# Opening of a hybrid decoder block on one core: norm weights spread by a 128-row product, fewer steps to the first norm factors, v's first weights cast on GpSimd and VectorE

## Chip, cores and metric

One core of a Trainium2 chip runs the whole program. The metric is the device time of one execution in microseconds (us), lower is better. Of the kernel before, three executions were timed (1725.62 to 1727.33, median 1726.06), and a further one was profiled.

## The reference

One decoder layer on x of 1024 tokens by 1024 channels, in float32. Two token mixers run side by side on the same normed input and are merged with gates; a SwiGLU channel mixer follows. Cut to what the change touches, and what hangs on it:

```python
def rms_norm(x, w):
    xf = x.astype(jnp.float32)
    y = xf * lax.rsqrt(jnp.mean(xf * xf, axis=-1, keepdims=True) + EPS)
    return (y * w.astype(jnp.float32)).astype(x.dtype)
...
h = rms_norm(x, attn_norm_w[l])
proj = h @ w_in[l]
q, k, v, u, g = jnp.split(proj, splits, axis=-1)
...
x = x + (g_a * y_a + g_b * y_b) @ w_out[l]
h = rms_norm(x, ffn_norm_w[l])
gt, up = jnp.split(h @ w_gate_up[l], 2, axis=-1)
x = x + (jax.nn.silu(gt) * up) @ w_down[l]
```

The change lies in the first norm of this, `rms_norm(x, attn_norm_w)`, and in the first piece of the product with w_in: the 256 columns of v that are computed first.

## The kernel before

**Tiling.** The 1024 tokens are eight tiles of 128 rows (`xts[0]` to `xts[7]`). A tile is loaded, its rows are squared and summed (`squares`), the sums become factors 1/sqrt(mean + EPS) (`roots`, through `rstd_of` and `rsq`), the rows are multiplied by factor and norm weight (`norm`, L714), and TensorE transposes them in 128x128 blocks into PSUM (`turn_x`, L724). All products are made to float32 accuracy out of two parts of each operand: a high part, which is a cast to fp32r (`split_hi`, ScalarE, L120), and a low part, the rest (`split_lo`, VectorE, L125). So three products stand for one: high by high, low by high, high by low. `hT_hi` and `hT_lo` are the transposed tile's two parts, and `low_x` makes the second.

**The opening.** `opening()` runs the first 50 us or so. While tiles arrive one by one, it computes the first 256 columns of v for tile after tile (`v_tile`, L1110): 24 products of 128x256 for each tile, eight of each of the three kinds. For tile 0 their order is hT_hi by v's high weights, hT_lo by the high weights, hT_hi by the low weights. v's weights come in two halves of 512 rows (`raws[0]`, `raws[1]`, each 128x1024 in the memory on chip), with high parts `wv[0][0]`, `wv[1][0]` (tile name vwh) and low parts `wv[0][1]`, `wv[1][1]` (vwl). Before, ScalarE casts both high parts (`wv_hi`, L120), VectorE subtracts for the first low part (L125) and GpSimd for the second (L1137). Behind `v_tile(1)` and the next ones follow u's first weights and the long rest of the program.

**What sets the order.** The list handed to `steps` is the order: each entry is issued behind the last instruction issued so far on VectorE, ScalarE and TensorE (`in_order`, with `after`), so these three engines work in the order of the list. GpSimd isn't tied by it; its instructions run in their own order as soon as what they wait for is there. A tile's buffer or a weight buffer is loaded anew when its last reader has finished. Loads are issued by SyncE, ScalarE or GpSimd, each with a queue of its own in which transfers follow one another.

**The norm weights.** `attn_norm_w` is one row of 1024. It is loaded into row 0 of `wb` (tile anw_b, L199), and `spread_weights(g)` (L212, L213) multiplies a column of ones with 512 of it, a product over one row, and copies the result from PSUM over all 128 rows of `wb`. `keep_busy(n)` (L208) issues n products of a tile of ones, whose results nobody reads.

**The first factors.** For tile 0 ScalarE squares and sums the first 512 columns (L699) and VectorE the other 512 (L700), and an addition joins both sums (L703). `rstd_of` scales by 1/D and adds EPS (L682); `rsq` takes a square root on ScalarE (L652), a reciprocal on VectorE (L653) and four more VectorE steps (L654 to L657): one Newton step. For the other tiles ScalarE squares all 1024 columns (L696).

Of the kernel before, what the change touches and what calls it, by code (L numbers as in the profile page):

```python
# [10 lines left out]
F32 = mybir.dt.float32  # L11
F32R = mybir.dt.float32r
AF = mybir.ActivationFunctionType
ALU = mybir.AluOpType
AX = mybir.AxisListType

P = 128
S = 1024
D = 1024
# [7 lines left out]
EPS = 1e-6  # L27
# [30 lines left out]
def kernel(  # L58
# [27 lines left out]
    nc = tc.nc  # L86
    dve, act, pool, pe = nc.vector, nc.scalar, nc.gpsimd, nc.tensor
# [11 lines left out]
    sm = ctx.enter_context(tc.tile_pool(name="sm", bufs=4))  # L99
# [12 lines left out]
    def nm(s):  # L112
        uid[0] += 1
        return f"{s}_{uid[0]}"

    def f32(ap):
        return ap.bitcast(F32)

    def split_hi(dst, src):
        act.copy(dst, src)  # L120
# [3 lines left out]
    def split_lo(dst, src, hi):  # L124
        last_lo[0] = dve.tensor_tensor(dst, src, f32(hi), op=ALU.subtract).ins  # L125
# [64 lines left out]
        queue.dma_start(xts[i][:], xs[i * P : (i + 1) * P, :])  # L190


    one = ap.tile([1, P], F32, name="one", bufs=1)
    busy = ap.tile([P, 512], F32R, tag="vl", name="busy")
    dve.memset(f32(busy[:]), 1.0)
    dve.memset(one[:], 1.0)
    wb = ap.tile([P, D], F32, name="anw_b", bufs=1)
    anw = [wb[0:1, 512 * g : 512 * (g + 1)] for g in range(2)]
    nc.scalar.dma_start(wb[0:1, :], attn_norm_w[:, :])  # L199
    xts[0] = ap.tile([P, D], F32, tag="xt", name="xt0", bufs=4)  # L200
    for g, queue in enumerate((nc.sync, nc.scalar)):
        queue.dma_start(xts[0][:, 512 * g : 512 * (g + 1)], xs[0:P, 512 * g : 512 * (g + 1)])
# [441 lines left out]
    def rsq(v, n, fast):  # L644

        r = sm.tile([P, 16], F32, tag="r", name=nm("r"))[:, :n]
        t = sm.tile([P, 16], F32, tag="t", name=nm("t"))[:, :n]
        if fast:
            act.activation(t, v, AF.Ln)
            act.activation(r, t, AF.Exp, scale=-0.5)  # L650
        else:
            act.activation(t, v, AF.Sqrt)  # L652
            dve.reciprocal(r, t)  # L653
        dve.tensor_tensor(t, r, r, op=ALU.mult)  # L654
        dve.scalar_tensor_tensor(t, v, 3.0e38, t, op0=ALU.min, op1=ALU.mult)
        dve.tensor_scalar(t, t, -0.5, 1.5, op0=ALU.mult, op1=ALU.add)
        dve.tensor_tensor(r, r, t, op=ALU.mult)  # L657
        return r
# [21 lines left out]
    def rstd_of(ss, n, scale, fast=False):  # L680
        v = sm.tile([P, 16], F32, tag="v", name=nm("v"))[:, :n]
        dve.tensor_scalar(v, ss, scale, EPS, op0=ALU.mult, op1=ALU.add)  # L682
        return rsq(v, n, fast)
# [5 lines left out]
    def squares(tiles):  # L689

        ss = sqs[tiles] = sm.tile([P, 4], F32, tag="ssx", name=nm("ssx"), bufs=2)[:, : len(tiles)]
        for j, i in enumerate(tiles):
            junk = ap.tile([P, D], F32, tag="junk", name=nm("xj"), bufs=1)
            src = xts[i]
            if i:
                act.activation(junk[:], src[:], AF.Square, accum_out=ss[:, j : j + 1])  # L696
            else:
                s2 = sm.tile([P, 1], F32, tag="ss", name=nm("ss"), bufs=1)
                act.activation(junk[:, :512], src[:, :512], AF.Square, accum_out=ss[:, j : j + 1])  # L699
                dve.tensor_tensor_reduce(  # L700
                    junk[:, 512:], src[:, 512:], src[:, 512:], 1.0, 0.0, ALU.mult, ALU.add, accum_out=s2[:]
                )
                dve.tensor_tensor(ss, ss, s2[:], op=ALU.add)  # L703

    def roots(tiles):

        r = rstd_of(sqs.pop(tiles), len(tiles), 1.0 / D)
        for j, i in enumerate(tiles):
            rx[i] = r[:, j : j + 1]

# [19 lines left out]
    def low_x(i):  # L730
        for g in range(2):
            src4, h_ = turned.pop((i, g))
            split_lo(hT_lo[:, 4 * g : 4 * g + 4, i * P : (i + 1) * P], src4, h_)
# [350 lines left out]
    def opening():  # L1084
# [10 lines left out]
        halves = [[t_[:].rearrange("p (k c) -> p k c", c=256) for t_ in w] for w in wv]  # L1095
        uw, o = [], {}

        def wv_hi(g):
            split_hi(wv[g][0][:], raws[g][:])

        def v_tile(i, first=0, n=24):

            if i % 2 == 0 and not first:
                o[i // 2] = pg()
            ts, dst = slice(i * P, (i + 1) * P), o[i // 2][:, 256 * (i % 2) : 256 * (i % 2 + 1)]
            order = ((0, 0), (0, 1), (1, 0)) if i else ((0, 0), (1, 0), (0, 1))
            terms = [(k, a_, b_) for a_, b_ in order for k in range(NKT)]
            for n_, (k, a_, b_) in list(enumerate(terms))[first : first + n]:
                l_, r_ = (hT_hi, hT_lo)[a_][:, k, ts], halves[k // 4][b_][:, k % 4, :]
                last_mm[0] = pe.matmul(dst, l_, r_, start=n_ == 0, stop=n_ == len(terms) - 1).ins  # L1110
# [9 lines left out]
        def turn_low(i):  # L1120
# [9 lines left out]
            lambda: spread_weights(1),  # L1130
            lambda: norm(0),
            lambda: keep_busy(1),
            lambda: wv_hi(0),
            lambda: split_lo(wv[0][1][:], raws[0][:], wv[0][0][:]),
            lambda: turn_x(0, (0,)),
            lambda: wv_hi(1),
            lambda: pool.tensor_tensor(wv[1][1][:], raws[1][:], f32(wv[1][0][:]), op=ALU.subtract),  # L1137
            lambda: turn_x(0, (1,)),
            lambda: low_x(0),
            lambda: v_tile(0),  # L1140
            lambda: squares((1,)),
            lambda: roots((1,)),
# [996 lines left out]
```

## Time and profile before

| What | Value |
|---|---|
| time of the profiled execution | 1724.98 us |
| span from its first to its last instruction | 1723.2 us |
| median of three other executions | 1726.06 us (1725.62, 1726.06, 1727.33) |
| TensorE (PE) busy | 1713.9 us, 99% of the span |
| VectorE (DVE) busy | 1276.2 us, 74% |
| ScalarE (ACT) busy | 873.2 us, 51% |
| GpSimd (POOL) busy | 219.2 us, 13% |
| transfers | 281.64 MB, 163 GB/s on average |

How to read it: busy shares are those of one execution, with times in us from the span's start. The 1.78 us by which the execution is longer than its span lie around the program's instructions. Matmuls overlap, and their ends are modelled, so TensorE's busy share doesn't tell how close it is to its peak; the distance from one matmul's start to the next does. A row of the timeline gives start, length, engine, line of the kernel, operation, operands, and in brackets the idle time before it and what ended that. The chain that ended last is found from the last instruction backwards, each time to what released it. A line such as L125 is that of a helper, so the operands' names tell which step it is.

### The profile page before, as it was taken

What the parts mean: (1) busy time and instruction counts of PE and PEld (TensorE: products, weight loads), DVE (VectorE), ACT (ScalarE), POOL (GpSimd) and SP (SyncE); (2) the same over time, 40 slices, a digit from 0 to 9 for tenths busy, and PEclk for the clock granted to TensorE, in tenths of its full rate; (3) what the DMA queues carried; (4) which work ended last, traced back from release to release, by engine and by line L of the source; (5) the groups of instructions that cost most, each with busy time, mean ns of one, the idle gap of its engine ahead of it and who ended that gap; (6) DMA issues with size and microseconds to landing.
All of it is one profiled execution on the core that took longest, in us unless ns stands there. A gap on an engine that the chain in (4) does not pass through costs nothing.

```text
span 1723.2 us, 25849 instructions
## 1 busy us (share of the span) xinstructions
PE 1713.9 (99%) x9243; PEld 1478.2 (86%) x9243; DVE 1276.2 (74%) x2128; ACT 873.2 (51%) x1958; POOL 219.2 (13%) x207
## 2 busy tenths in 40 slices
PE   9999999999999999999999999999999999999999
PEld 7997889998998998988788888888888888888887
DVE  7675889898988987977677769966666666575544
ACT  6333335767877886865556325633333333333332
POOL 4997851000000000000000000000000000000000
PEclk9999999999999999999999999999999999999999
DMA  6344445436345345354863683244455445597663
GB/s 209 117 128 134 131 151 143 113 103 174 107 128 147 116 125 148 99 146 145 316 225 128 196 301 108 77 141 156 149 174 167 153 143 165 175 371 271 216 217 128
DMA packets 261603, 281.64 MB, mean 163 GB/s; under 512 B 16545, under 2 KB 181985, under 8 KB 261474
## 3 DMA queue, kind: packets, MB, share of 16 engines
q1 hardware_dynamic: 254160, 267.71, 48.4%
q0 software_dynamic: 5680, 9.39, 2.6%
q10 hardware_dynamic: 1634, 2.89, 0.5%
q8 instruction: 73, 1.20, 0.3%
q14 instruction: 56, 0.46, 0.1%
HBM read 181.84 MB, written 85.50 MB: 155 GB/s over the span
## 4 chain that ended last, share of the span: by engine, by line
PE 93%; DVE 2%; DMA 2%; ACT 1%; issue 1%; SPq 0%; DVEq 0%; ACTq 0%
PE acc L984 30%; PE acc L488 12%; PE pg L168 12%; PE pg L170 12%; PE pg L169 12%; PE wo L1854 3%; PE sc L1294 2%; PE sc L1293 2%; PE pT L1332 2%; DVE acc L594 1%; PE pg L1110 1%; PE pW L168 1%; PE pW L170 1%; PE pW L169 1%; PE pQ L819 1%; DMA room<-in_w_out_dram 1%
## 5 line engine op out<-in xcount | busy, mean ns | idle before, releaser
L594 DVE SCALAR_TENSOR_TENSOR acc<-u,cw,acc 128x1023 f32<-128x1023 f32 (+14 forms) x240 | 303.5, 1264 | 23.0 <-ACT acc L588 20.4
L168 PE MATMUL pg<-whi,hT_hi 128*128 128x256 f32 x704 | 199.2, 284 | 0.8 <-DVE v L125 0.8
L169 PE MATMUL pg<-wlo,hT_hi 128*128 128x256 f32 x704 | 199.9, 284 | 0.0
L170 PE MATMUL pg<-whi,hT_lo 128*128 128x256 f32 x704 | 199.9, 284 | 0.0
L125 DVE TENSOR_TENSOR wlo<-draw,whi 128x1024 fp32r<-128x1024 f32 x75 | 91.8, 1224 | 86.0 <-ACT whi L120 78.6
L120 ACT CAST whi<-draw 128x1024 fp32r<-128x1024 f32 x75 | 79.1, 1055 | 129.5 <-PE acc L488 121.0
L168 PEld LDWEIGHTS pg<-whi,hT_hi 128*128 128x128 f32 x704 | 133.8, 191 | 2.6 <-DVE v L125 1.0
L169 PEld LDWEIGHTS pg<-wlo,hT_hi 128*128 128x128 f32 x704 | 134.2, 191 | 1.7
L170 PEld LDWEIGHTS pg<-whi,hT_lo 128*128 128x128 f32 x704 | 134.3, 191 | 1.5
L120 ACT CAST whi<-wraw 128x1024 fp32r<-128x1024 f32 x90 | 94.7, 1053 | 71.1 <-PE pg L169 37.0
L488 PE MATMUL acc<-wlo,whi 128*128 128x512 f32 x308 | 119.8, 389 | 0.0
L488 PE MATMUL acc<-whi,wlo 128*128 128x512 f32 x308 | 119.8, 389 | 0.0
L168 PE MATMUL pg<-hT_hi,whi 128*128 128x512 f32 x288 | 114.5, 398 | 0.0
L170 PE MATMUL pg<-hT_hi,wlo 128*128 128x512 f32 x288 | 113.9, 395 | 0.0
L169 PE MATMUL pg<-hT_lo,whi 128*128 128x512 f32 x288 | 113.9, 395 | 0.0
L1300 ACT ACTIVATE E<-E,mn 128x640 f32<-128x640 f32 (+7 forms) x128 | 99.5, 777 | 26.0 <-DVE mn L1295 25.6
L120 ACT CAST whi<-s 128x1024 fp32r<-128x1024 f32 x54 | 56.8, 1053 | 105.1 <-PE acc L984 102.0
L125 DVE TENSOR_TENSOR wlo<-wraw,whi 128x1024 fp32r<-128x1024 f32 x75 | 93.3, 1246 | 14.4 <-ACT whi L120 14.2
L984 PE MATMUL acc<-h_hi,whi 128*128 128x512 f32 x240 | 93.4, 389 | 0.0
L984 PE MATMUL acc<-h_lo,whi 128*128 128x512 f32 x240 | 93.4, 389 | 0.0
L1295 DVE CUSTOM_DVE_ANT_0 E<-sc,tb 128x512 f32<-128x512 f32 (+3 forms) x128 | 74.2, 585 | 23.6 <-PE pT L1332 13.8
L984 PE MATMUL acc<-h_hi,wlo 128*128 128x512 f32 x240 | 90.1, 389 | 0.0
(370 smaller groups left out, 4591.6 us busy)
## 6 DMA issues: line engine op xcount, KB each, us to landing
wraw<-in_w_gate_up_dram SPq DMA_DIRECT2D x44, 512.0 KB, 4.6
wraw<-in_w_in_dram SPq DMA_DIRECT2D x38, 512.0 KB, 4.1
qs<-qs SPq DMA_DIRECT2D x96, 128.0 KB, 2.3
wd<-in_w_down_dram SPq DMA_DIRECT2D x44, 256.0 KB, 3.1
tdT<-wd SPq DMA_DIRECT2D x88, 128.0 KB, 4.4
draw<-sdS SPq DMA_DIRECT2D x44, 256.0 KB, 3.8
draw<-tdT SPq DMA_DIRECT2D x44, 256.0 KB, 3.5
wraw<-in_w_in_dram SPq DMA_DIRECT2D x32, 256.0 KB, 3.2
```

What stands on the lines that cost most here:

```text
L120: act.copy(dst, src)
L125: last_lo[0] = dve.tensor_tensor(dst, src, f32(hi), op=ALU.subtract).ins
L168: pe.matmul(o, lh, rh, start=start, stop=False)
L169: pe.matmul(o, lh, rl, start=False, stop=False)
L170: last_mm[0] = pe.matmul(o, ll, rh, start=False, stop=stop).ins
L488: m = pe.matmul(o[s_][i][:], l_[:, ts], r_[:, 512:], start=start and j + y_ == 0, stop=j == n - 1 and y_ == 2, skip_group_check=not start,)
L594: dve.scalar_tensor_tensor(a_, us[c][:, : S - n], cw[:, c, t : t + 1], a_, op0=ALU.mult, op1=ALU.add)
L984: last_mm[0] = pe.matmul(o[:], a_[x_][:, k, :], b_[y_][:, k, :], start=start and k + x_ + y_ == 0, stop=k == 3 and x_ == 1, skip_group_che ...
L1293: pe.matmul(o[:, :w], qh[:, qs], k, start=True, stop=False)
L1295: dve.tensor_tensor_reduce(e[:, ks], o[:, :w], tb[:, S - nk + c0 : S - nk + c0 + w], 1.0, mn[:, j : j + 1] if c0 else 3.0e38, ALU.add, ALU ...
L1300: act.activation(e[:, :nk], e[:, :nk], AF.Exp, bias=mn[:, j : j + 1], scale=-1.0, accum_out=l[:, j : j + 1])
L1854: last_mm[0] = pe.matmul(o[s_][i][:], A[u_], B[v_], start=start and j + y_ == 0, stop=j == 3 and y_ == 2, skip_group_check=not start,).ins
```

## The change

Five things, all in the opening:

- *Spreading the norm weights.* `one` becomes a 128x128 tile that is zero but for row 0, which holds ones. The weights' row is loaded 32 times, into rows 0 to 31 of `wb`, by one transfer of 128 KB in place of 4 KB, and rows 32 to 127 are set to zero, the first 512 columns by VectorE, the others by GpSimd. The product then runs over all 128 rows and gives the same sums.
- *Joining tile 0's sums.* ScalarE's half is scaled while it squares, EPS is added to its sum, and VectorE's reduction of the other half starts from that value, so it ends with mean + EPS. The addition of L703 and the step of L682 fall away for tile 0; VectorE's reduction now waits for ScalarE's sum.
- *Shorter Newton step for a single column* (tiles 0 and 1): w = -v/2 is made beside the square root, and two steps follow the reciprocal in place of four.
- *Casts of v's first weights.* GpSimd casts the first half, VectorE the second, and ScalarE none.
- *Low parts of v's first weights.* GpSimd subtracts for the whole first half, VectorE and GpSimd for 512 columns each of the second; these now stand behind `low_x(0)` in the list.

```diff
-    one = ap.tile([1, P], F32, name="one", bufs=1)
+    one = ap.tile([P, P], F32, name="one", bufs=1)
     busy = ap.tile([P, 512], F32R, tag="vl", name="busy")
     dve.memset(f32(busy[:]), 1.0)
-    dve.memset(one[:], 1.0)
+    dve.memset(one[:], 0.0)
+    dve.memset(one[0:1, :], 1.0)
     wb = ap.tile([P, D], F32, name="anw_b", bufs=1)
-    anw = [wb[0:1, 512 * g : 512 * (g + 1)] for g in range(2)]
-    nc.scalar.dma_start(wb[0:1, :], attn_norm_w[:, :])
+    anw = [wb[:, 512 * g : 512 * (g + 1)] for g in range(2)]
+    nc.scalar.dma_start(wb[0:32, :], attn_norm_w.to_broadcast([32, D]))
+    for g, eng in enumerate((dve, pool)):
+        for r0, n in ((64, 64), (32, 32)):
+            eng.memset(wb[r0 : r0 + n, 512 * g : 512 * (g + 1)], 0.0)
...
             act.activation(t, v, AF.Sqrt)
+            if n == 1:
+                w = sm.tile([P, 1], F32, tag="w", name=nm("w"), bufs=1)
+                dve.tensor_scalar(w[:], v, 3.0e38, -0.5, op0=ALU.min, op1=ALU.mult)
             dve.reciprocal(r, t)
+            if n == 1:
+                dve.scalar_tensor_tensor(t, r, w[:], r, op0=ALU.mult, op1=ALU.mult)
+                dve.scalar_tensor_tensor(r, t, 1.5, r, op0=ALU.add, op1=ALU.mult)
+                return r
...
-                s2 = sm.tile([P, 1], F32, tag="ss", name=nm("ss"), bufs=1)
-                act.activation(junk[:, :512], src[:, :512], AF.Square, accum_out=ss[:, j : j + 1])
+                v = sm.tile([P, 16], F32, tag="v", name=nm("v"))[:, :1]
+                act.activation(junk[:, :512], src[:, :512], AF.Square, scale=D**-0.5, accum_out=ss[:, j : j + 1])
+                dve.tensor_scalar(ss, ss, EPS, None, op0=ALU.add)
                 dve.tensor_tensor_reduce(
-                    junk[:, 512:], src[:, 512:], src[:, 512:], 1.0, 0.0, ALU.mult, ALU.add, accum_out=s2[:]
+                    junk[:, 512:], src[:, 512:], src[:, 512:], 1.0 / D, ss, ALU.mult, ALU.add, accum_out=v
                 )
-                dve.tensor_tensor(ss, ss, s2[:], op=ALU.add)
+                sqs[tiles] = v
...
-        def wv_hi(g):
-            split_hi(wv[g][0][:], raws[g][:])
+        def wv_low(eng, e):
+            es = slice(512 * e, 512 * (e + 1))
+            eng.tensor_tensor(wv[1][1][:, es], raws[1][:, es], f32(wv[1][0][:, es]), op=ALU.subtract)
...
             lambda: keep_busy(1),
-            lambda: wv_hi(0),
-            lambda: split_lo(wv[0][1][:], raws[0][:], wv[0][0][:]),
+            lambda: pool.tensor_copy(wv[0][0][:], raws[0][:]),
+            lambda: dve.tensor_copy(wv[1][0][:], raws[1][:]),
             lambda: turn_x(0, (0,)),
-            lambda: wv_hi(1),
-            lambda: pool.tensor_tensor(wv[1][1][:], raws[1][:], f32(wv[1][0][:]), op=ALU.subtract),
             lambda: turn_x(0, (1,)),
             lambda: low_x(0),
+            lambda: pool.tensor_tensor(wv[0][1][:], raws[0][:], f32(wv[0][0][:]), op=ALU.subtract),
+            lambda: wv_low(dve, 0),
+            lambda: wv_low(pool, 1),
             lambda: v_tile(0),
```

VectorE's queue from the norm of tile 0 (xt_102, the product of both halves) to the first step of tile 1's factor, before; wraw is a raw weight half, px the transposed tile in PSUM:

```order
L714 SCALAR_TENSOR_TENSOR xt_102<-xt_102,r_360,anw_b 128x512 x2
L125 TENSOR_TENSOR vwl_341<-wraw_334,vwh_340 128x1024
L125 TENSOR_TENSOR hT_lo<-px_380,hT_hi 128x4x128
L125 TENSOR_TENSOR hT_lo<-px_388,hT_hi 128x4x128
L682 TENSOR_SCALAR v_424<-ssx_421 128x1
```

The same piece of VectorE's queue in the changed kernel, where tile 0 is xt_107 and the raw halves are wraw_339 and wraw_340:

```order
L727 SCALAR_TENSOR_TENSOR xt_107<-xt_107,r_363,anw_b 128x512 x2
L1148 CAST vwh_347<-wraw_340 128x1024
L125 TENSOR_TENSOR hT_lo<-px_383,hT_hi 128x4x128
L125 TENSOR_TENSOR hT_lo<-px_389,hT_hi 128x4x128
L1113 TENSOR_TENSOR vwl_348<-wraw_340,vwh_347 128x512
L693 TENSOR_SCALAR v_428<-ssx_425 128x1
```

The first half's subtraction has left VectorE; a cast of the second half stands in its place, and half a subtraction behind the two low parts of tile 0, ahead of tile 1's factor.

GpSimd's queue from the making of the identity matrix to its next memset (the vectors' rows), before:

```order
masks.py:197 MEMSET ident 128x128
masks.py:199 ISA
masks.py:199 AFFINE_SELECT ident<-ident 128x128
L1137 TENSOR_TENSOR vwl_343<-wraw_335,vwh_342 128x1024
L230 MEMSET rows 64x128
```

and in the changed kernel:

```order
masks.py:197 MEMSET ident 128x128
L203 MEMSET anw_b 64x512
L203 MEMSET anw_b 32x512
masks.py:199 ISA
masks.py:199 AFFINE_SELECT ident<-ident 128x128
L1147 CAST vwh_345<-wraw_339 128x1024
L1152 TENSOR_TENSOR vwl_346<-wraw_339,vwh_345 128x1024
L1113 TENSOR_TENSOR vwl_348<-wraw_340,vwh_347 128x512
L234 MEMSET rows 64x128
```

Two memsets have come ahead of the identity's last step, and a cast and a subtraction of the first half plus half a subtraction of the second stand where one subtraction stood. ScalarE's queue is the same but for the two weight casts, which are gone, and TensorE's order is unchanged.

More of the change, by code (lines that the diff above doesn't have):

```diff
@@ L697, in squares @@
             else:
-                s2 = sm.tile([P, 1], F32, tag="ss", name=nm("ss"), bufs=1)
-                act.activation(junk[:, :512], src[:, :512], AF.Square, accum_out=ss[:, j : j + 1])
+                v = sm.tile([P, 16], F32, tag="v", name=nm("v"))[:, :1]
+                act.activation(junk[:, :512], src[:, :512], AF.Square, scale=D**-0.5, accum_out=ss[:, j : j + 1])
+                dve.tensor_scalar(ss, ss, EPS, None, op0=ALU.add)
                 dve.tensor_tensor_reduce(
-                    junk[:, 512:], src[:, 512:], src[:, 512:], 1.0, 0.0, ALU.mult, ALU.add, accum_out=s2[:]
+                    junk[:, 512:], src[:, 512:], src[:, 512:], 1.0 / D, ss, ALU.mult, ALU.add, accum_out=v
                 )
-                dve.tensor_tensor(ss, ss, s2[:], op=ALU.add)
+                sqs[tiles] = v
     def roots(tiles):
-        r = rstd_of(sqs.pop(tiles), len(tiles), 1.0 / D)
+        ss = sqs.pop(tiles)
+        r = rsq(ss, 1, False) if tiles == (0,) else rstd_of(ss, len(tiles), 1.0 / D)
         for j, i in enumerate(tiles):
```

## The prediction

> **What bounds the kernel now.** I read the page first: the busy shares, then the chain that ended last.
>
> ```profile
> PE 1713.9 (99%) x9243; PEld 1478.2 (86%) x9243; DVE 1276.2 (74%) x2128; ACT 873.2 (51%) x1958; POOL 219.2 (13%) x207
> ...
> PE 93%; DVE 2%; DMA 2%; ACT 1%; issue 1%; SPq 0%; DVEq 0%; ACTq 0%
> ```
>
> TensorE is the bound almost throughout. Then TensorE's waits over the whole span (who, for whom: us in total, times, longest); behind the wait of its very first instruction the longest is this:
>
> ```profile
> PE pg L168 <- DVE v L125: 0.8, 1, 0.8
> ```
>
> A wait of 0.8 us is the longest, so no later stage has slack that could swallow a delay: whatever the opening gains or loses goes to the end one for one. The change touches only the first 15 us, so I read there the chain that ended last, in order of time (start, length, what; DVE is VectorE, ACT ScalarE, POOL GpSimd):
>
> ```profile
> 1.31 3.22 DMA xt<-in_x_dram
> ...
> 4.56 0.69 DVE xj L700
> ...
> 5.37 0.17 DVE ssx L703
> ...
> 5.75 0.21 ACT t L652
> ...
> 5.98 0.17 DVE r L653
> ...
> 6.76 0.17 DVE r L657
> ...
> 7.02 0.76 DVE xt L714
> ...
> 7.92 1.10 PE px L724 x4
> ...
> 9.04 0.59 ACT hT_hi L120
> 9.63 0.29 ACT vwh L120
> ...
> 10.47 0.59 ACT hT_hi L120
> 11.06 1.06 ACT xj L696 x2
> ...
> 13.67 1.41 DVE xt L714 x2
> ...
> 22.56 0.87 PE px L724 x8
> ```
>
> Tile 0 is squared, gets its factor, is normed (7.02), transposed and cast; ScalarE's weight cast (9.63) holds back the second cast (10.47); then tile 1 is squared on ScalarE and normed on VectorE from 13.67. What follows hangs on that norm, so I measure the change at one point: **when the norm of tile 1 starts, 13.67 now.**
>
> **Shorter factor steps.** In the chain, the add at 5.37 and the EPS step behind it disappear between the reduction and the square root: the root can start about 0.38 sooner (two steps of 0.19, from 5.37 to 5.75). Of the four steps between the reciprocal's end (6.15) and the norm (7.02), the last of them the row at 6.76, two remain, and each takes 0.19 to 0.20 with its hand-over: 0.39 less. The new step w fits into the 0.23 between root and reciprocal (5.75 to 5.98). Together 0.77 for tile 0, and 0.39 for tile 1, which only loses the two later steps. The second reduction now waits for ScalarE's sum, which is there before its own data.
>
> **The weight rows by DMA.** 31 more rows of 4 KB, 124 KB, stand ahead of half of x and of v's weights in ScalarE's queue. The stage's rate (last number, GB/s), the issue of v's two weight halves (the second at about 2.2), and the time from issue to landing of the first and of the second:
>
> ```profile
> 8.00:14.50 6.50, 6.29 (x32) 5.70 (x33) 4.93 (x12) 5.58 (x10) 3.84 (x5) 1.00 0.96 331
> ...
> 1.71 1.00 ACTq L1089 DMA_DIRECT2D wraw<-in_w_in_dram  x2
> ...
> wraw<-in_w_in_dram ACTq DMA_DIRECT2D x1, 512.0 KB, 5.2
> ...
> wraw<-in_w_in_dram ACTq DMA_DIRECT2D x1, 512.0 KB, 6.2
> ```
>
> At 331 GB/s the rows cost 0.37 us; I take 0.4 (bounds: 0, if they fit into idle engines, and 0.5 at a slower start). Every later landing moves by it: weights at 7.3 and 8.8 in place of 6.9 and 8.4. The norm of tile 0 starts at 7.02 - 0.77 + 0.4 = 6.65, its first half ends at 7.4.
>
> **Memsets and the product over 128 rows.**
>
> ```profile
> 0.92 0.48 DVE L195 MEMSET busy<- 128x512 f32 x1 [0.92 <-PEq L2125]
> ...
> 3.03 3.77 PE L212 MATMUL pm<-anw_b,one 1*128 1x512 f32 x4
> 6.84 0.59 ACT L213 COPY anw_b<-pm 128x512 f32<-128x512 f32 x1 [0.42 <-PE pm L212]
> ```
>
> VectorE's extra memsets (about 0.48 twice, two small ones) end by 2.7, before the product at 3.03. GpSimd's two start by 1.0; at the price per column of its 128-column step further below (0.29) they take at most 1.2 each and end by 3.4, and only the second product, from about 4.9, needs them. Neither costs anything. The product has the same four passes and may start up to 0.4 later with its rows, so the second copy ends between 7.43 and 7.8, and the second half of norm 0 can start at 7.5 or later. What 128 rows may buy is TensorE's rate: four transposes took 1.10 here and eight took 0.87 at 22.56. An earlier fast rate would save about 0.65 per four transposes, but only ahead of waits that VectorE and GpSimd end, below.
>
> **The casts.** ScalarE loses both weight casts: the second cast of hT_hi no longer waits (10.47 could become about 9.9). But GpSimd now has a cast, a product-sized subtraction and half of another, and VectorE a cast and half a subtraction, at the same time. Rows where both engines worked at once:
>
> ```profile
> 11.09 0.69 DVE L125 TENSOR_TENSOR hT_lo<-px,hT_hi 128x512 fp32r<-128x512 f32 x1 [0.74 <-ACT hT_hi L120]
> 12.76 0.29 DVE L654 TENSOR_TENSOR t<-r 128x1 f32<-128x1 f32 x1
> ...
> 48.75 4.78 DVE L272 TENSOR_TENSOR lprod<-lamt 128x64 f32<-128x64 f32 x2
> 54.15 1.68 DVE L264 TENSOR_SCALAR pvec<-pvec 128x8 f32<-128x8 f32 x1
> 56.66 2.57 DVE L125 TENSOR_TENSOR wlo<-wraw,whi 128x1024 fp32r<-128x1024 f32 x1
> ...
> 46.34 9.46 POOL L900 TENSOR_TENSOR F<-hT_hi,hT_lo 128x1024 f32<-128x1024 f32 x4
> 55.76 9.08 POOL L909 TENSOR_TENSOR F<-F,F 128x1024 f32<-128x1024 f32 x3
> ```
>
> Two products of 64 columns took 2.4 us each, the length of a GpSimd instruction (9.46 / 4); the subtraction at 56.66 took 2.57, and the GpSimd rows beside it 3.03 each. So a VectorE instruction with two SBUF operands waits until GpSimd's current one ends, runs, and holds up GpSimd's next. Even a one-column step (12.76) took 0.29. The subtraction at 11.09, with one operand in PSUM, ran 0.69 in the midst of a GpSimd subtraction: it isn't held. The prices:
>
> ```profile
> L1750 DVE TENSOR_SCALAR fnw_b<-fnw_b 128x1024 f32<-128x1024 f32 x1 | 0.7, 681 | 0.0
> L125 DVE TENSOR_TENSOR wlo<-draw,whi 128x1024 fp32r<-128x1024 f32 x75 | 91.8, 1224 | 86.0 <-ACT whi L120 78.6 <-DMA xr<-x_d 3.0 <-DMA wd<-in_w_down_dram 1.5
> ...
> L1137 POOL TENSOR_TENSOR vwl<-wraw,vwh 128x1024 fp32r<-128x1024 f32 x1 | 2.4, 2385 | 9.3 <-ACT vwh L120 9.3
> L131 POOL TENSOR_TENSOR sl<-wraw,sh 128x512 fp32r<-128x512 f32 x7 | 9.1, 1303 | 1.6 <-ACT sh L120 1.6
> L1184 POOL COPY seen<-xt 128x1 f32<-128x1 f32 x1 | 0.2, 186 | 13.3 <-DVE xt L714 13.3
> masks.py:199 POOL TENSOR_SCALAR_AFFINE_SELECT ident<-ident 128x128 f32<-128x128 f32 x1 | 0.3, 294 | 0.1
> ```
>
> VectorE's cast: 0.68 (one operand) to 1.22 (a subtraction of that size); I take 0.68, its likeness. GpSimd's cast: the two one-operand rows differ by 0.108 for 127 columns, so 1024 columns make about 1.05; the upper bound is the subtraction, 2.39. I take 1.05.
>
> Now the queues, instruction by instruction, with norm steps and half subtractions of 0.7 on VectorE. GpSimd's cast is ready at 7.3, in the middle of norm 0. **Order A:** it waits for both halves: cast 8.2 to 9.25; VectorE's cast, ready since 8.8, 9.25 to 9.95; GpSimd's subtraction 9.95 to 12.35; meanwhile VectorE's two hT_lo steps (not held) end at 11.3; VectorE's half 12.35 to 13.0; GpSimd's half 13.0 to 14.3; the factor of tile 1, begun at 13.0, reaches its first two-operand step at 13.65, waits until 14.3, and the norm starts at 14.7: **+1.0**. **Order B:** GpSimd's cast slips in between the halves: 7.4 to 8.45, norm 0's second half 8.45 to 9.2, GpSimd's subtraction 9.2 to 11.6, VectorE's cast 11.6 to 12.3, both hT_lo to 13.5, VectorE's half behind GpSimd's (13.6) to 14.3, norm 1 at about 15.35: **+1.7**. **Order C:** as B, but a cast that isn't held: 9.2 to 10.4, hT_lo to 11.7, halves to 12.35 and 13.65, norm 1 at 14.05: **+0.4**. TensorE cannot hide it: tile 0's last products need GpSimd's half (14.3 in A), and then it waits for norm 1 as now.
>
> What decides between C and the others is whether an SBUF cast is held. The Trainium skill, "SBUF — State Buffer", section "Who interferes with whom", says that copies and casts can run in a two-port mode and then contend with GpSimd as two-operand steps do, whoever starts first keeping the pair. By it C falls away and the shift is +1.0 to +1.7; the trace agrees as far as it goes, with the 1.68 us of L264, which has one operand.
>
> Other queues: SyncE's load of u's first weights waits for the last reader of v's first half, now GpSimd (12.35 in A), and x tile 5 stands behind it.
>
> ```profile
> wraw<-in_w_in_dram SPq DMA_DIRECT2D x2, 512.0 KB, 5.7
> ...
> 20.20 1.06 ACT L120 CAST whi<-wraw 128x1024 fp32r<-128x1024 f32 x1
> ```
>
> They land 5.7 us behind that, at about 18.1, and ScalarE casts them at 20.20, itself later by the shift: 2 us of cover. GpSimd's vector loads start behind its last weight step (14.3), and the first of them is used at 48.75.
>
> **The sum.** +1.0 us, against the profiled execution's 1724.98: 1725.98. That execution lies 1.08 below the median of the three runs, 1726.06, and 0.64 below the lowest, so for a median I forecast 1727.0 (rounded). A measurement of this kernel can tell about 0.2% (3.45 us) from no change: this forecast is "no change". Chance 0.64.
>
> **Rivals.** *A small gain:* the two engines don't hold each other up here. Then VectorE casts at 8.8 to 9.5, both hT_lo end at 10.8, its half at 11.4; ScalarE squares tile 1 behind its cast (9.9) in 1.06, so by 11.1; the factor's steps take 1.05, norm 1 starts at 12.45, -1.2: 1723.8 by the profiled execution, 1724.9 by the median. For it speaks that the chain of now runs through ScalarE, which the change frees; against it the 2.57, 4.78 and 1.68 above. 0.28.
>
> *Slower:* GpSimd's cast costs what its subtraction does, 2.39. Everything behind it in order A is 1.34 later: norm 1 at +2.3. TensorE then has long idle stretches up to 16 and may stay at its slow rate: 16 products of tile 1 at twice 0.14 (2.30 for 16 at 15.92 in the chain below) add up to 2.3.
>
> ```profile
> 15.92 2.30 PE pg L1110 x16
> ```
>
> That makes up to +4.6, 1730.7 by the median. It decides from about 3.45 on, so it needs both the dear cast and most of the slow rate. Against it: the one-operand rows, and that 128-row products should rather raise the rate early. The Trainium skill, "TensorE: Matmul & The Clock Gate", Part 1, says that the half rate is the resting state, left after some 3.4 us of activity and entered again after an idle window. By it both directions are open; the trace agrees only in part, as TensorE was active from 1.46 and its transposes at 7.92 were still slow. 0.08.
>
> *Not as it says:* the 128 rows change nothing in TensorE's rate. That moves neither case, since GpSimd and VectorE end the waits; it is inside the forecast.
>
> **Range and chances.** Low end: the gain on the profiled execution, 1723.8, less 0.2 of scatter: 1723.6. High end: the highest run, 1727.33, with order B's +1.7: 1729.0. Outside lie most of the slow rival and little else. Faster by over 0.2%: 0.02, since no case reaches it without luck; slower: 0.06, the greater part of that rival; within: 0.92.
>
> **What would show it.** Right: in the changed trace VectorE's cast or half subtraction is far longer than 0.7 and ends with a GpSimd row; norm 1 starts after 14; ScalarE's second hT_hi cast comes before 10.4. Wrong: all of VectorE's rows at their usual lengths and norm 1 at 12.5; or GpSimd's cast at 2 us or more; or transposes at the fast rate early and TensorE without waits before 14.

## The result, and the profile after

| | before | after |
|---|---|---|
| median of 12 executions | 1725.77 us (1723.87 to 1732.72) | 1730.11 us (1729.70 to 1732.09) |
| span of the profiled execution | 1723.2 us | 1728.3 us |
| ratio after to before | | 1.0026, interval [1.0018, 1.0034] |

The kernel became slower by 4.3 us, 0.26%. The forecast was 1727.0 and "no change", with 1729.0 as its high end: it was wrong.

The shares of the changed kernel say nothing of it; TensorE is as full as before:

```profile
PE 1715.8 (99%) x9243; PEld 1477.1 (85%) x9243; DVE 1279.6 (74%) x2129; ACT 871.3 (50%) x1956; POOL 222.7 (13%) x211
...
PE 94%; DVE 2%; DMA 2%; ACT 1%; issue 1%; SPq 0%; DVEq 0%; ACTq 0%
```

**The opening** comes first, since the prediction lived there. Norm 0, the norm of tile 0, in the timeline before (start, length):

```profile
7.02 1.41 DVE L714 SCALAR_TENSOR_TENSOR xt<-xt,r,anw_b 128x512 f32<-128x512 f32 x2
```

And after, with what VectorE and GpSimd do around it:

```profile
7.07 1.06 POOL L1147 CAST vwh<-wraw 128x1024 fp32r<-128x1024 f32 x1 [4.62 <-DMA wraw<-in_w_in_dram]
7.32 4.11 DVE L727 SCALAR_TENSOR_TENSOR xt<-xt,r,anw_b 128x512 f32<-128x512 f32 x2
...
8.21 2.66 POOL L1152 TENSOR_TENSOR vwl<-wraw,vwh 128x1024 fp32r<-128x1024 f32 x1
...
11.35 0.68 DVE L1148 CAST vwh<-wraw 128x1024 fp32r<-128x1024 f32 x1
...
12.11 1.28 POOL L1113 TENSOR_TENSOR vwl<-wraw,vwh 128x512 fp32r<-128x512 f32 x1 [1.23 <-DVE vwh L1148]
...
15.53 1.42 DVE L727 SCALAR_TENSOR_TENSOR xt<-xt,r,anw_b 128x512 f32<-128x512 f32 x2
```

And from the chain that ended last in the profile after, in order of time:

```profile
0.76 3.65 DMA anw_b<-in_attn_norm_w_dram
...
4.54 3.58 PE pm L216 x4
...
8.15 0.59 ACT anw_b L217
...
8.77 2.67 DVE xt L727
...
12.64 0.60 ACT hT_hi L120
```

The two halves of norm 0 took 4.11 us in place of 1.41. The first (1.35, alone 0.75) stood beside GpSimd's cast. The second started at 8.77, behind the copy of the second half of the spread weights, when GpSimd's subtraction was under way; that one ended at 8.21 + 2.66 = 10.87, and the norm at 11.44. So the norm of tile 1 starts at 15.53 in place of 13.67, +1.86. The prediction had +1.0, and 15.35 in its order B. Each of these starts is that of one execution: with the same queues the norm of tile 1 starts at 14.52 in run 1 below and at 15.19 in run 3.

**The rest of the kernel** is the news. The same five products of TensorE, found by their place in its sequence, in the timeline before: the first of u, one near the end of the first stage, one of the output projection, one early in the second stage, and the very last. The first and the second stage are two long stretches of products into `acc` (L984, after L997). Some of their operands are the high and low parts (h, l) of the tiles T1 to T4, which are sums of blocks of the normed input, and of one block of the weights (sh, sl).

```profile
27.10 0.40 PE L168 MATMUL pg<-hT_hi,whi 128*128 128x512 f32 x1
...
244.99 0.39 PE L984 MATMUL acc<-hT_hi,whi 128*128 128x512 f32 x1
...
1020.07 0.39 PE L1854 MATMUL wo<-whi,mTh 128*128 128x512 f32 x1
...
1164.94 0.39 PE L984 MATMUL acc<-h_lo,whi 128*128 128x512 f32 x1
...
1718.92 0.39 PE L488 MATMUL acc<-whi,wlo 128*128 128x512 f32 x1
```

And after:

```profile
29.20 0.40 PE L168 MATMUL pg<-hT_hi,whi 128*128 128x512 f32 x1
...
249.52 0.39 PE L997 MATMUL acc<-hT_hi,whi 128*128 128x512 f32 x1
...
1023.61 0.39 PE L1869 MATMUL wo<-whi,mTh 128*128 128x512 f32 x1
...
1168.40 0.39 PE L997 MATMUL acc<-h_lo,whi 128*128 128x512 f32 x1
...
1724.02 0.39 PE L492 MATMUL acc<-whi,wlo 128*128 128x512 f32 x1
```

The shift is 2.10, 4.53, 3.54, 3.46 and 5.10. The opening gave 2.1; the first stage (110 to 245) added 2.4, the middle gave back 1.0, the second stage (1165 to 1530) added 1.6. No instruction of those stages was changed. Groups of TensorE by form show which products grew (the number behind the comma is the mean ns of one). Before, in 110 to 245, then in 1165 to 1530:

```profile
L984 PE MATMUL acc<-hT_lo,whi 128*128 128x512 f32 x81 | 31.5, 389 | 0.0
L984 PE MATMUL acc<-T2h,whi 128*128 128x512 f32 x28 | 10.9, 389 | 0.0
...
L984 PE MATMUL acc<-T4h,sl 128*128 128x512 f32 x76 | 29.6, 389 | 0.0
L984 PE MATMUL acc<-T2h,whi 128*128 128x512 f32 x72 | 28.0, 389 | 0.0
```

After, the same:

```profile
L997 PE MATMUL acc<-hT_lo,whi 128*128 128x512 f32 x79 | 30.8, 390 | 0.0
L997 PE MATMUL acc<-T2h,whi 128*128 128x512 f32 x28 | 11.1, 396 | 0.0
...
L997 PE MATMUL acc<-T4h,sl 128*128 128x512 f32 x76 | 30.1, 396 | 0.0
...
L997 PE MATMUL acc<-T2h,whi 128*128 128x512 f32 x72 | 28.0, 389 | 0.0
```

In the first stage the products with T2h grew by 7 ns each and those with hT_lo did not; in the second stage those with sl grew, and those with T2h did not. What the grown ones have in common is not an operation but a place; the runs below test it. The new tile `w` holds 4 bytes for each row and takes 32 in the small pool, and every pool that is laid out behind that one from the same end of the memory moves up by 32 bytes. In the compiled programs the first stage's T tiles (which stream through TensorE) move, and in the second stage sh and sl (which are loaded as its weights) do, while hT, whi, wlo and the second stage's T tiles stay. Before, all of them begin on multiples of 256 bytes: T2h at 156160, now 156192. The kernel has a tile of 128 bytes in the small pool that nothing reads (`pad_sm`, L107); its size is part of what sets this place.

Not every product whose operands moved grew. In the attention, between the two stages, both operands of 480 products of 128x256 (`pW`) move off their multiples of 256 by the same 32 bytes. Their groups read the same in both profiles, this one word for word, and in both they start 120 ns apart at the median:

```profile
L168 PE MATMUL pW<-ph,vh 128*128 128x256 f32 x160 | 45.7, 286 | 0.1
```

So a cost of the place is seen in products of 128x512 alone. Why the narrower ones are free of it, the runs don't show.

### The profile page after: what moved, and what is told of

Its sections match the earlier page's. It is cut to its first block, busy times and chain, and to the rows that moved or that the text cites. A ratio compares the mean times of both kernels' runs of the same rounds, so it can differ in the third digit from the quotient of the medians.

```text
span 1728.3 us, 25855 instructions
## 1 busy us (share of the span) xinstructions
PE 1715.8 (99%) x9243; PEld 1477.1 (85%) x9243; DVE 1279.6 (74%) x2129; ACT 871.3 (50%) x1956; POOL 222.7 (13%) x211
## 4 chain that ended last, share of the span: by engine, by line
PE 94%; DVE 2%; DMA 2%; ACT 1%; issue 1%; SPq 0%; DVEq 0%; ACTq 0%
PE acc L997 30%; PE acc L492 12%; PE pg L168 12%; PE pg L169 12%; PE pg L170 12%; PE wo L1869 3%; PE sc L1309 2%; PE sc L1308 2%; PE pT L1347 2%; DVE acc L598 1%; PE pg L1124 1%; PE pW L168 1%; PE pW L170 1%; PE pW L169 1%; PE pQ L832 1%; DMA room<-in_w_out_dram 1%
## 5 line engine op out<-in xcount | busy, mean ns | idle before, releaser
L997 PE MATMUL acc<-h_lo,whi 128*128 128x512 f32 x240 | 93.4, 389 | 0.0
L997 PE MATMUL acc<-h_hi,whi 128*128 128x512 f32 x240 | 93.4, 389 | 0.0
L997 PE MATMUL acc<-h_hi,wlo 128*128 128x512 f32 x240 | 90.2, 389 | 0.0
```

What stands on the lines that cost most here:

```text
L997: last_mm[0] = pe.matmul(o[:], a_[x_][:, k, :], b_[y_][:, k, :], start=start and k + x_ + y_ == 0, stop=k == 3 and x_ == 1, skip_group_che ...
```

## The experiments

Each ran beside executions of the kernel before, on the same chip; the ratio is to those, and it isn't exactly the quotient of the medians. "u" is the start of u's first product in the profile (27.10 before). It depends on when the second half of x's first tile has landed, and that differs from one profile to the next: in five profiles with the opening of before (the kernel before itself, and it with the moves of runs 2 to 4) it landed at 4.53, 5.30, 4.81, 5.04 and 5.88, and u came 22.55 to 22.58 us behind it each time. So the 27.10 is the earliest of five, the others lie at 27.37 to 28.44, and where it matters u is counted from this landing.

**1. The change without the move.** `w` takes the place of another small tile:

```diff
-                w = sm.tile([P, 1], F32, tag="w", name=nm("w"), bufs=1)
+                w = sm.tile([P, 1], F32, tag="ss", name=nm("w"), bufs=1)
```

> The whole change, but the new one-column tile w takes the place of the small tile that the change has freed, so that no buffer allocated after it moves; in the change they moved by 32 bytes. Theory (moved buffers): of the 4.3 us that the change costs, about 2.4 come from products in the Strassen-like stages whose operands moved by 32 bytes; they go, so about 1727.7, ratio to before about 1.001; the starts of acc<-T4h,sl products lie 227 ns apart as before and not 233; norm 1 still starts at about 15.5. Rival (all of it is the opening and what follows from it): no change against the changed kernel, 1730.1, ratio 1.0025.

Measured: 1726.27 us, before 1725.27, ratio 1.0000 [0.9992, 1.0009]; that is below the 1727.7 expected, and the norm of tile 1 starts at 14.52, not at 15.5. The grown groups are back at their old length, in 110 to 245 and in 1165 to 1530:

```profile
L997 PE MATMUL acc<-T2h,whi 128*128 128x512 f32 x28 | 10.9, 389 | 0.0
...
L997 PE MATMUL acc<-T4h,sl 128*128 128x512 f32 x76 | 29.6, 389 | 0.0
```

The loss of the changed kernel goes with the place of `w`; all five intended changes together are worth no more than a measurement's uncertainty.

**2. The move without the change**, by 32 bytes, then by 64:

```diff
-    sm.tile([P, 32], F32, name="pad_sm", bufs=1)
+    sm.tile([P, 40], F32, name="pad_sm", bufs=1)
...
-    sm.tile([P, 32], F32, name="pad_sm", bufs=1)
+    sm.tile([P, 48], F32, name="pad_sm", bufs=1)
```

> The kernel before, with a padding tile 32 bytes longer and nothing else, so that the same buffers move by 32 bytes as in the change. Theory (moved buffers): about 2.4 us slower than before (1728.2, ratio 1.0014), with acc<-T4h,sl 233 ns apart, and an opening as before (norm 1 at 13.7). Rival (all is the opening): no difference from before, 1725.8.

> The kernel before, with the same padding tile 64 bytes longer. If what costs is that the operands no longer start on a multiple of 64 bytes: no difference from before, 1725.8, products 227 ns apart. If any move away from the old addresses costs: as with 32 bytes, about 1728.2. If the opening alone is the cause: no difference either, so this run tells only between the first two.

Measured: 32 bytes 1729.69, ratio 1.0020 [1.0010, 1.0030]; 64 bytes 1727.87, ratio 1.0014 [1.0005, 1.0023]; before 1725.27. One unread tile that is 32 bytes longer costs as much as the whole change did, and more than the 2.4 expected: in its profile the first stage takes 2.5 longer and the second 1.6. A multiple of 64 isn't enough.

**3. 128 bytes, and the change with 256.** First in the kernel before, then in the changed kernel (224 bytes more, with the 32 of `w` 256):

```diff
-    sm.tile([P, 32], F32, name="pad_sm", bufs=1)
+    sm.tile([P, 64], F32, name="pad_sm", bufs=1)
...
-    sm.tile([P, 32], F32, name="pad_sm", bufs=1)
+    sm.tile([P, 88], F32, name="pad_sm", bufs=1)
```

> The kernel before with a pad that moves the same later buffers by 128 bytes (32 and 64 bytes have been run). Theory, a product reads its operand slower when the buffer does not begin on a multiple of some number of bytes: if that number is 128, the products of the first and second stage start 227 ns apart again and the time equals before's, 1725.3 to 1725.8, ratio 1.000; if it is 256, they start at 229 to 233 ns and the time is 2 to 3 us above, ratio 1.0010 to 1.0016. Rival, what counts is how far the buffers lie from their old place, whatever the multiple: then the products are as slow as at 64 bytes or slower, 231 ns and more.

> The changed kernel, complete with its new tile, and 224 bytes of padding more, so that all later buffers stand 256 bytes from where they were before, on multiples of 256 again. Theory of the multiple: the products start 227 ns apart as before, and what is left is the opening alone, so the time is that of the changed kernel without the moved buffers, about 1726.3, ratio 1.000 to 1.001. Rival, the place itself (the distance from other buffers, a later end of the pools): products at 234 ns and 1730, ratio 1.0025.

Measured: 128 bytes 1729.81, ratio 1.0026 [1.0015, 1.0036]; the change with 256 bytes 1726.42, ratio 1.0007 [0.9998, 1.0016]; before 1725.11. Products overlap, so their distance is read from starts: the first and the last of twelve in a row in the first stage. Moved by 128:

```profile
178.05 0.39 PE L984 MATMUL acc<-T4h,sh 128*128 128x512 f32 x1
...
180.62 0.40 PE L984 MATMUL acc<-T4h,sl 128*128 128x512 f32 x1
```

The change, moved by 256:

```profile
178.57 0.39 PE L997 MATMUL acc<-T4h,sh 128*128 128x512 f32 x1
...
181.06 0.39 PE L997 MATMUL acc<-T4h,sl 128*128 128x512 f32 x1
```

2.57 us over eleven distances is 234 ns; 2.49 is 226. The rival (the place itself, or how far the buffers moved) falls: the farthest move is the free one. Of the four moves tried, only the one by 256 costs nothing that shows: 1726.42 stands beside the 1726.27 of run 1, which moves nothing.

**4. One pool alone.** 32 bytes ahead of sh and sl of the second stage only, in the kernel before:

```diff
     fp = fp_ctx.enter_context(tc.tile_pool(name="fp", bufs=2, reuse_waits="tile"))
+    fp.tile([P, 8], F32, name="pad_fp", bufs=1)
```

> The kernel before with 32 bytes of padding at one later place only, so that of the moved buffers only the weight sums sh and sl of the second stage (1165 to 1530 us) stand off their multiple of 256; all of the first stage stands as before. Theory of the multiple: products with T4 and sh or sl in the second stage go from 227 to 232 to 234 ns, some 250 of them, +1.6 to 1.8 us, all others stay at 227; time 1726.8 to 1727.1, ratio 1.0010. Rival, the slowing comes with the move of many buffers together (say, of those that engines write beside TensorE's reads), not from the operand's own place: no product changes, ratio 1.000.

Measured: 1726.96, before 1725.14, ratio 1.0011 [1.0002, 1.0020]. In 110 to 245, then in 1165 to 1530:

```profile
L984 PE MATMUL acc<-T2h,whi 128*128 128x512 f32 x28 | 10.9, 390 | 0.0
...
L984 PE MATMUL acc<-T4h,sl 128*128 128x512 f32 x76 | 30.1, 396 | 0.0
```

Only the products whose own operand moved grew: 3 x 76 of them in the second stage, at 7 ns 1.6 us. That operand is the one loaded as weights; in the first stage of run 2 it was the streamed one. Each alone is enough.

**5. The casts put back**, in the version of run 1 (casts and low parts as in the kernel before):

```diff
-            lambda: pool.tensor_copy(wv[0][0][:], raws[0][:]),
-            lambda: dve.tensor_copy(wv[1][0][:], raws[1][:]),
+            lambda: split_hi(wv[0][0][:], raws[0][:]),
+            lambda: split_lo(wv[0][1][:], raws[0][:], wv[0][0][:]),
...
+            lambda: split_hi(wv[1][0][:], raws[1][:]),
+            lambda: pool.tensor_tensor(wv[1][1][:], raws[1][:], f32(wv[1][0][:]), op=ALU.subtract),
...
-            lambda: pool.tensor_tensor(wv[0][1][:], raws[0][:], f32(wv[0][0][:]), op=ALU.subtract),
-            lambda: wv_low(dve, 0),
-            lambda: wv_low(pool, 1),
```

> As the first (no moved buffers), and the casts and low parts of v's first weights made where they were before (ScalarE casts, VectorE and GpSimd subtract); the 128-row product, its 32-row load and the short factor steps stay. Theory (VectorE and GpSimd hold each other up): norm 1 starts at about 14.1 in place of 15.5, because what is left is the later landing of x and of the weight rows; about 1726.3, some 1.4 less than the first run. Rival (the casts cost nothing, the later landings make the delay): as the first run, norm 1 at 15.5, 1727.7.

Measured: 1724.56, before 1725.27, ratio 0.9994 [0.9985, 1.0002]; u at 27.55, against 28.26 in run 1. It is 1.7 us below run 1, where 1.4 was expected, and the eleven executions of each hardly overlap (1724.05 to 1725.40, and 1725.35 to 1727.09): so the new casts cost time, though neither version can be told from the kernel before. With GpSimd idle, norm 0 isn't held any more:

```profile
7.18 0.75 DVE L727 SCALAR_TENSOR_TENSOR xt<-xt,r,anw_b 128x512 f32<-128x512 f32 x1
...
8.84 0.75 DVE L727 SCALAR_TENSOR_TENSOR xt<-xt,r,anw_b 128x512 f32<-128x512 f32 x1 [0.91 <-ACT anw_b L217]
...
13.91 1.42 DVE L727 SCALAR_TENSOR_TENSOR xt<-xt,r,anw_b 128x512 f32<-128x512 f32 x2
```

But its second half still waits, for the copy of the spread weights: 0.91 us.

**6. Without the rows, and the factor steps alone.** From run 1, the weights' row and its product as before (one row); then also the edit of run 5:

```diff
-    one = ap.tile([P, P], F32, name="one", bufs=1)
+    one = ap.tile([1, P], F32, name="one", bufs=1)
...
-    nc.scalar.dma_start(wb[0:32, :], attn_norm_w.to_broadcast([32, D]))
-    for g, eng in enumerate((dve, pool)):
-        for r0, n in ((64, 64), (32, 32)):
-            eng.memset(wb[r0 : r0 + n, 512 * g : 512 * (g + 1)], 0.0)
...
+    nc.scalar.dma_start(wb[0:1, :], attn_norm_w[:, :])
```

> The changed kernel without the moved buffers, and with the norm weights spread as before (one row loaded, product over one row): casts on GpSimd and VectorE and the shorter factor steps remain. Theory, the 124 KB of rows delay x: tile 0's halves land near 3.6 and 4.5 in place of 4.6 and 5.1, the first norm starts near 6.3 in place of 7.3, and the norm of tile 1 up to 0.8 earlier than the 14.5 with the rows; TensorE then runs at the slow rate till about 13, as before. Time 0.3 to 0.8 below the 1726.3 with the rows. Rival, the early fast rate of the 128-row product is worth more than the delay: transposes and v's first products cost more without it, so that u's first product comes at 28.5 or later in place of 28.3, and the time is 0.3 to 1 above 1726.3.

> The kernel before with the shorter factor steps alone (no rows, no product over 128 rows, casts as before, no moved buffers). By the prediction's terms the factor of tile 0 comes 0.77 earlier and that of tile 1 0.39: norm 0 near 6.25, norm 1 between 12.9 and 13.3, u's first product 0.4 to 0.8 before 27.1, time 1724.6 to 1725.0, ratio 0.9996. Rival, ScalarE's weight cast and second cast of hT_hi (9.63 to 11.06) wait for v's weights, which land at 6.9 and 8.4 whatever the factors do, so only the 0.39 of tile 1 or less is seen: ratio 0.9998 to 1.000. If it is as fast as the version with the rows and the casts put back (0.9994), the rows and the product over 128 rows are worth nothing.

Measured, before 1725.11: without the rows 1725.60, ratio 1.0000 [0.9991, 1.0009], u at 28.30; the steps alone 1724.82, ratio 0.9999 [0.9990, 1.0008], u at 26.70. The steps alone start the norm of tile 1 at 13.07, 0.60 earlier, and u 0.40 earlier, though the second half of x's first tile landed 0.37 later here (4.90, before 4.53). Counted from that landing, u comes 0.77 earlier (21.80, before 22.57). With the casts added, that half lands at 4.87 and u is 1.6 later; the timeline of that version shows a part of why:

```profile
8.50 2.68 POOL L1148 TENSOR_TENSOR vwl<-wraw,vwh 128x1024 fp32r<-128x1024 f32 x1
...
8.88 2.85 DVE L1144 CAST vwh<-wraw 128x1024 fp32r<-128x1024 f32 x1
...
14.63 1.42 DVE L723 SCALAR_TENSOR_TENSOR xt<-xt,r,anw_b 128x512 f32<-128x512 f32 x2
```

VectorE's cast, 0.68 us when it ran alone in the changed kernel, took 2.85 beside GpSimd's subtraction and ended 0.55 behind it. The Trainium skill, "SBUF — State Buffer", section "Who interferes with whom", counts casts among what can contend with GpSimd; this row agrees. Orders A and B of the prediction rested on it.

**7. VectorE's cast given to ScalarE**, in the version without the rows:

```diff
-            lambda: dve.tensor_copy(wv[1][0][:], raws[1][:]),
             lambda: turn_x(0, (0,)),
             lambda: turn_x(0, (1,)),
+            lambda: split_hi(wv[1][0][:], raws[1][:]),
```

> The version without the rows and without the moved buffers (casts on GpSimd and VectorE, shorter factor steps), with VectorE's cast of v's second half given to ScalarE, behind the second cast of hT_hi; GpSimd keeps its cast and its subtractions. Theory, the casts cost because VectorE's cast stands held behind GpSimd's subtraction (8.88 to 11.73 in the version with it) and both hT_lo steps and all that follows stand behind the cast: without it hT_lo ends by 11.5 and not 12.9, VectorE's half subtraction by 12.5, and the norm of tile 1 starts at 13.5 to 13.9 in place of 14.63; u's first product 0.5 to 1.2 before 28.30, time 1724.4 to 1725.1. Rival, the length of GpSimd's own chain (cast, subtraction, half subtraction) sets v's first tile and the norm behind it whatever VectorE does: norm of tile 1 at 14.3 or later, u's first product at 28.0 or later.

Measured: 1725.74, before 1724.54, ratio 1.0011 [1.0002, 1.0020]; norm of tile 1 at 13.92, u at 27.89, span 1723.5. From its timeline:

```profile
12.83 1.91 PE L1120 MATMUL pg<-vwh,hT_lo 128*128 128x256 f32 x8
```

The norm came 0.71 earlier, as the theory had it, but u only 0.41 (0.5 to 1.2 expected): eight products took 1.91, against 1.30 in the version with VectorE's cast. Eight at a granted clock of 0.50 took 2.25 in the changed kernel (at 12.25), so by that length most of them ran at TensorE's slow rate; the granted clock of that stretch reads 1.00, as it does in the slow first 12 us of the kernel before, so the length alone speaks for it. And the time didn't fall. The held cast is a real cost, but not the whole of the 1.6; the rest of it isn't settled.

**8. Cheaper rows.** From run 5, the 128 KB issued behind x; then, from that, one row only, into zeros:

```diff
-    nc.scalar.dma_start(wb[0:32, :], attn_norm_w.to_broadcast([32, D]))
...
         queue.dma_start(xts[0][:, 512 * g : 512 * (g + 1)], xs[0:P, 512 * g : 512 * (g + 1)])
+    nc.scalar.dma_start(wb[0:32, :], attn_norm_w.to_broadcast([32, D]))
```

```diff
+    pool.memset(wb[0:32, :], 0.0)
...
-    nc.scalar.dma_start(wb[0:32, :], attn_norm_w.to_broadcast([32, D]))
+    nc.scalar.dma_start(wb[0:1, :], attn_norm_w[:, :])
```

> The changed kernel without the moved buffers and with the casts as before, and the 128 KB transfer of weight rows issued behind tile 0's second half in ScalarE's queue instead of ahead of it. Theory, the rows cost by standing ahead of x: both halves of tile 0 land at 3.6 to 4.5 again (4.4 and 4.9 with the rows ahead), the rows themselves by 4.7, and the opening is 0.3 to 0.8 shorter than with the rows ahead (u's first product at 26.8 to 27.3 in place of 27.55); time 1724.0 to 1724.6. Rival, the copies of the spread weights hold norm 0 anyway (second copy at 8.2 because the two products over 128 rows start only with the rows): no gain, u's first product at 27.5 or later.

> As the run beside it, but only one row of weights is loaded (4 KB) into a tile that is zero in the other 127 rows, so the product over 128 rows stays and the 124 KB go. Theory, what is good in the change is the factor steps and the early fast rate of TensorE, what is bad the 124 KB and the casts: x lands as before (3.6 and 4.5), the product over 128 rows starts by 3.7, TensorE reaches the fast rate by 9 and keeps it, u's first product comes at 26.3 to 26.7 (27.1 before, 26.7 with the factor steps alone); time 1724.3 to 1724.9, ratio 0.9995 to 0.9998, which five rounds cannot tell from before. Rival, the early fast rate is worth nothing, because norm 0 and v's weights are waited for, not TensorE: u's first product at 26.7 or later.

Measured, before 1725.14: 1726.25, ratio 1.0006 [0.9997, 1.0015], u at 28.12; one row 1725.87, ratio 1.0005 [0.9996, 1.0014], u at 28.51. Both expectations failed. Behind x the rows land later (5.21), the two products start at 5.34 and at 5.67, and norm 0 waits for the copies of their results (8.04 and 8.43 in place of 7.18). The 4 KB were no better than the 128 KB, but they didn't stand in the same place: they waited for GpSimd's memset of the rows, and in ScalarE's queue they were issued at 1.85, behind half of v's first weights (1.19), where the 128 KB were issued at 1.19. So both runs show that norm 0 waits for the row, and not what its size costs. No version here beats the kernel before by more than its uncertainty.

## Why the prediction was wrong, point by point

- **"The change touches only the first 15 us."** This is the step that failed. It was read off the list of instructions, and the list is the same from 27 us on; but the change also makes a tile, and that moved operands of 576 later products of 128x512 (28 of each of twelve kinds in the first stage, 80 of each of three in the second) off their multiple of 256. By the five products above the two stages grew by 2.43 and 1.64 us, 4.1 of the span's 5.1; runs 1 and 2 show it from both sides, 3 and 4 that it is the operand's own place. It needed no wait, so the view of TensorE's waits could not hint at it.
- **"No later stage has slack."** Nearly right: of the shift 1.0 went in the middle in the changed kernel, 0.2 to 0.4 in runs 1 and 3; in the profile of the 32-byte move it grew there by 0.5, and in that of the steps alone by 1.1. What the middle takes or gives is about what one execution differs from the next.
- **The opening, +1.0 (orders A to C, 0.4 to 1.7).** Near in size, and half right in mechanism. With the move undone the change costs 1.0 (run 1) and 1.3 us (run 3) by the medians, and both intervals include no change at all. The three profiles with the changed opening have u at 28.26, 28.87 and 29.20, 1.1 later on average than the five with the opening before, so the 2.1 of the single pair above holds about 1 us of chance. The two engines did hold each other up, as it said, but in none of its three orders: GpSimd's subtraction began before norm 0's second half, which waited for it, and VectorE's cast and half subtraction, which were to be the long rows, took 0.68 each.
- **The rows, 0.4 on every landing.** Mis-sized. Tile 0's first half landed 1.06 later (4.62, before 3.56), the second 0.56 (inside the scatter of the five profiles), v's weights by less than 0.1. The rows themselves landed at 4.41, so the products began 1.5 later (4.54, before 3.03), where the prediction had at most 0.4, and the second copy ended at 8.74, not by 7.8. Without GpSimd's work (run 5) norm 0's second half still waited 0.91 for it.
- **The factor steps, 0.77 and 0.39.** Right. From the end of VectorE's reduction to norm 0 it is 1.77 before and 0.99 with the steps alone (run 6), 0.78 less; from the end of tile 1's sum to its norm 1.56 and 1.18, 0.38 less. At u 0.77 of it is left.
- **GpSimd's cast 1.05, VectorE's 0.68, no cast free of the other engine.** Right: 1.06, 0.68, and 2.85 where it was held (run 6). In the changed kernel itself it was norm 0 that was held, and VectorE's cast came too late to meet GpSimd's subtraction.
- **ScalarE's second hT_hi cast before 10.4.** Wrong: 12.64, since norm 0's second half ended at 11.44. Of the three signs of being right, only the norm of tile 1 behind 14 came.
- **The slow rival, 1730.7.** Its time was close to the result, its mechanism wasn't what happened: GpSimd's cast was cheap. That it came near is luck.

The range was wrong because all its cases moved the same 15 us. A case "something outside the change moves" wasn't among them.

## What to carry to other kernels

When a change creates, removes or resizes a tile, compare the addresses of the operands of the hottest products before and after, in the compiled programs; a padding tile that seems to do nothing may be what holds them. When a kernel loses time in stages that were not touched, group one engine's instructions by form, stage by stage, and look for the forms that grew by a few ns: the operand that they share is the lead. Work moved to an engine that looks idle isn't free: here GpSimd's cast and subtraction held up the norm that they were to run beside (4.11 us in place of 1.41). And read an opening from more than one profile, from a point that all of them share.

## What the runs showed of the hardware

- A product of 128x128 by 128x512 in fp32r starts 226 to 227 ns behind the one before, at the median, when both operands begin on a multiple of 256 bytes (first and second stage of the kernel before). With the streamed operand or the loaded weights 32 or 128 bytes off such a multiple it is 232 to 234 ns (runs 2 to 4); 64 bytes off it is 231 ns with the streamed operand and 233 with the weights (run 2). Products of 128x256 with both operands 32 bytes off stay at 120 ns (the attention, before and after). The Trainium skill, "SBUF — State Buffer", section "Operand start alignment", asks of an operand's start only a multiple of its element's size, and says that this is about what is legal, not about speed; all the moves here are legal by it, and three of four cost time. Why 256, the runs don't show.
- TensorE's fast rate came earlier with the product over 128 rows: tile 0's first four transposes took 0.63 to 0.87 in all profiles that have it (0.63 at 8.82 in the changed kernel), and 1.08 to 1.10 in all with the product over one row (1.10 at 7.92 before). In the changed kernel and in run 3 it was lost again behind norm 0's hold, in run 1, whose norm 0 was held too (its first half took 2.68), it wasn't. The same window before and after, granted clock third from the end:

```profile
11.20:14.63 3.43, 3.43 (x21) 3.35 (x22) 2.63 (x9) 3.18 (x7) 3.43 (x5) 1.00 0.95 289
...
11.20:14.63 3.43, 3.15 (x14) 3.03 (x15) 2.79 (x6) 1.64 (x3) 2.52 (x4) 0.50 0.31 87
```

- The landing of one and the same transfer at the start of the kernel, 256 KB of x, scattered by 1.35 us between five profiles with the same opening (4.53 to 5.88), and u's first product moved with it within 0.03. So a difference of under about 1 us between two openings, read from one profile each, is weak evidence unless it is counted from that landing. In the changed opening norm 0 waits for the rows and for GpSimd too, so the parts of its cost stay uncertain.
